# The ninth pair's up product by seven half products, weight sums of two pairs by DMA during the attention, and stores through GpSimd's queue

## The chip, the cores and the metric

The kernel runs on one core of one Trainium2 chip. The metric is device time in microseconds, from the start of the program to its end; before the change the runs took 647.18, 648.11 and 648.23 us, with a median of 648.11. TensorE (PE) multiplies; VectorE (DVE), ScalarE (ACT) and GpSimd (POOL) work elementwise; SyncE (SP) issues most DMAs. A DMA that GpSimd issues goes through a queue of its own, and it can add to its destination instead of overwriting it.

## The reference

One decoder layer over 512 tokens of width 1024, in float32:

```python
mix = fox_mixer(x, w_in, b_f, w_out)              # 16 heads of attention with forget gates
x = layer_norm(alpha * x + mix, g1, b1)
u, g = split(x @ w_up, 2816)                      # the up product: 1024 -> 2 x 2816
ffn = (gelu(causal_dwconv(g)) * u) @ w_down       # the down product: 2816 -> 1024
x = layer_norm(alpha * x + ffn, g2, b2)
out = x + sigmoid(x @ w_gate + b_gate) * (p @ w_proj)
```

Precision is kept by splitting each operand into a high and a low part (`hi` = the value rounded to the matmul's float32r form, `lo` = the rest) and adding three products: hi with hi, hi with lo, lo with hi.

## The kernel before, in words

**Stages.** The trace shows them in this order: the value, query and key projections with the attention, head by head (to about 226 us), the out projection and the first norm (to 247), the up and down products interleaved (247 to 566), the last down rows and the second norm (to 590), the gate with the embedding and the stores (to the end).

**Weights.** The class `Weights` holds a list of units, each up to 128x1024 numbers, in the order of their use. `load_to` issues a unit's load on SP's queue into one of four `raw` buffers (now and then into a piece of the tile `side`); `cut_to` splits it: ScalarE writes `whi` (L123), VectorE subtracts and writes `wlo` (L129), in five buffers each. `get(i, 4)` hands out unit i and first splits up to unit i + 4. A unit may have a `make`, sums of weights that VectorE forms before the split; `make` of the next unit runs ahead of the split of the present one.

**The up product in pairs.** F = 2816 is 22 rows of 128, in eleven pairs j = 0 to 10 (the "ninth pair" is j = 8, the "tenth" j = 9). For g and for u, a row done whole takes one unit and 24 products of 512 columns (`up`). A pair in `UP_PAIRS` takes a 2x2 block form with seven products of halves in place of eight (`up_step`): stages 0, 1, 2 are 24 products of 256 columns each, stage 3 is twelve, for g and u in turn. This form needs sums of x (`x_sums`, formed once, at L775) and four sums of the pair's weights. For pairs in `KEPT` (3, 4, 6, 7) VectorE forms these during the attention (`keep_sums`) and they are stored to DRAM (`keep_load`); for the other pairs in `UP_PAIRS` (2 and 9) VectorE forms them when the unit is due: `t12` two sums (L207, L208), `t3` one (L215), `t4` one (L222). Pairs outside `UP_PAIRS` need none.

**Operands of the down product.** After a pair's convolution and gate (`conv_product`: L759 to L768) its result E is summed (`operand_sums`, L855 to L858) and split (`operand_parts`, L863, L864) for the down product, which has a seven-product form as well, for three groups of three pairs (0 to 2, 3 to 5, 6 to 8). Where the next pair is in `APART`, this work waits until that pair's second unit; else it follows at once.

**The down product between the up units.** `down` yields twelve steps for a group: three each of ua, ub, uc, ud, one for each pair of the group. The first three kinds are twelve products of 512 columns, ud six; after the third of a kind, VectorE adds finished banks to the result (`give`, L661). `CHUNKS` says how many steps go to each of twelve (last group: eight) slots between the up units of the next group. The third step of a kind reads the operands of the group's last pair.

**Order.** From the up product's third row to the second norm, VectorE's and ScalarE's orders are the program's (`manual_schedule`). TensorE's order is made by a planner that takes, at each point of its own timeline, the first instruction of the program that it believes to be ready. A matmul that writes a bank waits until its last reader is done.

**Attention.** For each head, VectorE adds the mask and takes the maximum (L521), ScalarE exponentiates, GpSimd scales the four row blocks by the inverse sum (L533), and TensorE transposes them (L546) for the product with the values. GpSimd does nothing else there.

**The end.** `finish` forms a 128x512 piece of the output and stores it through SP's queue (L1107), which is also the queue of the gate weights' loads.

## Time and profile before

| | us |
|---|---|
| runs: 647.18, 648.11, 648.23, median | 648.11 |
| profiled execution | 648.06 |
| its span, first to last instruction | 646.4 |
| busy: TensorE / its weight loads / VectorE / ScalarE / GpSimd | 639.4 / 562.9 / 533.3 / 384.8 / 121.5 |
| DMA: 121.08 MB, mean rate | 187 GB/s |

A row of a group of instructions gives the line, the engine, the operation, what it writes and reads, the shape and count, then busy us and the mean in ns, and the idle time before it with what ended it. A row of a timeline begins with start and length in us. A matmul's length contains its way through the array; how often matmuls follow one another is read from their starts.

### The profile page before, as it was taken

The numbers are of one execution on the slowest core, as the hardware profiler recorded it, in microseconds if no ns is written. First come the engines' busy times: TensorE is split into PE (matmuls) and PEld (weight loads), VectorE is DVE, ScalarE is ACT, GpSimd is POOL, SyncE is SP. The second block draws the span as 40 slices with busy tenths as digits, with TensorE's granted clock in tenths as the row PEclk, the third lists the DMA queues.
The fourth block names the chain that finished last, engine by engine and source line by source line (L and its number), as shares of the span: only waits on it lengthen the run. The fifth ranks groups of instructions, "written<-read, shape, count | busy, mean of one in ns | idle before, by whom it ended". The sixth has DMA issues, their size and how long they took to land.

```text
span 646.4 us, 10081 instructions
## 1 busy us (share of the span) xinstructions
PE 639.4 (99%) x3630; PEld 562.9 (87%) x3630; DVE 533.3 (83%) x870; ACT 384.8 (60%) x685; POOL 121.5 (19%) x133
## 2 busy tenths in 40 slices
PE   9999999999999999999999999999999999999996
PEld 7899888888888889989999988999988998888885
DVE  7764779988888589857899897889797998699977
ACT  6643777877785316945756563646554555337863
POOL 0000554454456043110000010101010001002000
PEclk9999999999999999999999999999999999999999
DMA  8763525455588477685787849766846764671472
GB/s 296 239 235 131 204 83 175 166 186 158 178 280 305 133 254 219 137 209 156 198 223 160 223 128 247 196 204 149 249 132 184 192 213 143 167 243 33 139 228 98
DMA packets 49921, 121.08 MB, mean 187 GB/s; under 512 B 4880, under 2 KB 8720, under 8 KB 49872
## 3 DMA queue, kind: packets, MB, share of 16 engines
q1 hardware_dynamic: 45552, 108.92, 51.3%
q0 software_dynamic: 4320, 11.54, 10.6%
q8 instruction: 28, 0.46, 0.3%
q14 instruction: 21, 0.17, 0.1%
HBM read 107.72 MB, written 18.87 MB: 196 GB/s over the span
## 4 chain that ended last, share of the span: by engine, by line
PE 91%; DMA 3%; ACT 2%; DVE 2%; issue 1%; SPq 0%; ACTq 0%; DVEq 0%
PE g L152 18%; PE u L152 18%; PE pp L152 14%; PE x L152 8%; PE pv L152 7%; PE z L152 4%; PE r L152 3%; PE ap L152 3%; PE ao L152 3%; PE o L559 3%; PE t L546 3%; PE y L152 2%; PE s L509 2%; PE pl L152 2%; PE s L511 2%; DMA raw<-gt 2%
## 5 line engine op out<-in xcount | busy, mean ns | idle before, releaser
L123 ACT ACTIVATE whi<-raw 128x1024 fp32r<-128x1024 f32 (+4 forms) x141 | 132.6, 944 | 92.6 <-issue 12.9
L129 DVE TENSOR_TENSOR wlo<-raw,whi 128x1024 fp32r<-128x1024 f32 (+4 forms) x136 | 144.9, 1075 | 31.3 <-ACT whi L123 30.5
L533 POOL TENSOR_SCALAR pr<-pr,rl 128x128 f32<-128x128 f32 (+1 forms) x64 | 75.6, 1197 | 131.9 <-DVE rl L529 131.9
L280 POOL COPY neghalf<-neghalf 128x1 f32<-128x1 f32 x16 | 9.0, 562 | 247.0 <-ACT neghalf L279 247.0
L152 PE MATMUL g<-x1h,whi 128*128 128x256 f32 (+1 forms) x168 | 54.6, 325 | 0.0
L152 PE MATMUL g<-x1l,whi 128*128 128x256 f32 (+1 forms) x168 | 54.4, 324 | 0.0
L152 PE MATMUL g<-x1h,wlo 128*128 128x256 f32 (+1 forms) x168 | 54.3, 323 | 0.0
L152 PE MATMUL u<-x1l,whi 128*128 128x256 f32 (+1 forms) x160 | 52.9, 331 | 0.0
L152 PE MATMUL u<-x1h,wlo 128*128 128x256 f32 (+1 forms) x160 | 52.9, 331 | 0.0
L152 PE MATMUL u<-x1h,whi 128*128 128x256 f32 (+1 forms) x160 | 52.9, 331 | 0.0
L152 PE MATMUL pp<-xh,wlo 128*128 128x512 f32 x128 | 50.5, 395 | 0.0
L152 PE MATMUL pp<-xl,whi 128*128 128x512 f32 x128 | 50.0, 391 | 0.0
L152 PE MATMUL pp<-xh,whi 128*128 128x512 f32 x128 | 50.0, 390 | 0.0
L525 ACT ACTIVATE pr<-s,nm 128x128 f32<-128x128 f32 (+1 forms) x64 | 33.6, 528 | 9.1 <-DVE nm L521 8.9
L152 PEld LDWEIGHTS g<-x1h,whi 128*128 128x128 f32 x168 | 31.9, 190 | 3.4 <-issue 0.7
L152 PEld LDWEIGHTS g<-x1l,whi 128*128 128x128 f32 x168 | 31.9, 190 | 2.6
L152 PEld LDWEIGHTS g<-x1h,wlo 128*128 128x128 f32 x168 | 31.9, 190 | 2.6
L152 PEld LDWEIGHTS u<-x1h,whi 128*128 128x128 f32 x160 | 30.4, 190 | 3.0
L152 PEld LDWEIGHTS u<-x1l,whi 128*128 128x128 f32 x160 | 30.4, 190 | 2.9
L152 PEld LDWEIGHTS u<-x1h,wlo 128*128 128x128 f32 x160 | 30.4, 190 | 2.8
L123 ACT ACTIVATE whi<-side 128x512 fp32r<-128x512 f32 (+1 forms) x33 | 25.5, 782 | 11.0 <-DVE side L215 2.6
L521 DVE CUSTOM_DVE_ANT_0 s<-s,mask 128x128 f32<-128x128 f32 (+1 forms) x64 | 30.0, 512 | 1.7 <-PE s L511 1.5
(630 smaller groups left out, 1856.6 us busy)
## 6 DMA issues: line engine op xcount, KB each, us to landing
raw<-wup SPq DMA_DIRECT2D x34, 512.0 KB, 6.2
raw<-wdn SPq DMA_DIRECT2D x23, 512.0 KB, 4.6
raw<-wqk SPq DMA_DIRECT2D x16, 512.0 KB, 3.3
ka<-wup SPq DMA_DIRECT2D x8, 512.0 KB, 4.2
kb<-wup SPq DMA_DIRECT2D x8, 512.0 KB
kept<-kb SPq DMA_DIRECT2D x8, 512.0 KB, 3.4
kept<-ka SPq DMA_DIRECT2D x8, 512.0 KB, 3.1
raw<-wo SPq DMA_DIRECT2D x8, 512.0 KB, 4.4
```

Of the source, the lines that this page charges most:

```text
L123: self.nc.scalar.activation(hi[:, c:e], piece, AF.Copy)
L129: self.nc.vector.tensor_sub(lo[:, c:e], piece, hi[:, c:e].bitcast(F32))
L152: nc.tensor.matmul(ps, lhsT, rhs, start=start and n == 0, stop=stop and n == 2, skip_group_check=on)
L280: with tc.issue_after(nc.gpsimd.tensor_copy(small[:, m + 32:m + 33], small[:, m:m + 1]).ins):
L509: nc.tensor.matmul(ps[:, :n], QA[:, q], KA[:, :n], start=True, stop=False)
L511: nc.tensor.matmul(ps[:, :n], qb[0:68, q], kb[0:68, :n], start=False, stop=True)
L521: last_mask[:] = [nc.vector.tensor_tensor_reduce(ps[:, :w], ps[:, :w], mask[:, S - w:], -1.0, BIG, op0=ALU.add, op1=ALU.min, accum_out=nm[ ...
L525: nc.scalar.activation(pr[:, off:off + w], ps[:, :w], AF.Exp, bias=nm[:, i:i + 1], scale=-1.0, accum_out=ls[:, i:i + 1])
L533: nc.gpsimd.tensor_scalar_mul(pr[:, off:off + w], pr[:, off:off + w], rl[:, i:i + 1])
L546: nc.tensor.transpose(ps[:, w:w + P], pr[:, o:o + P], ident)
L559: nc.tensor.matmul(ps[:, q0:], V[:, j, h], p[:, o:o + w], start=j == 0 and n == 0, stop=j == NT - 1 and n == 1)
```

## The change

- Pair 8 joins `UP_PAIRS`: its up product takes the seven-product form. Pairs 8 and 9 join `APART`.
- Pairs 8 and 9 are in a new list `KEPT_DMA`. Their weight sums come from DRAM, like those of `KEPT`, but are formed by DMA: eight steps for each half of each pair, four copies and four accumulating DMAs of 256 KB, DRAM to DRAM. Two of these 32 are issued on GpSimd behind each head's scaling.
- An accumulating DMA only adds, so the signs of the weight sums of the up product turn from minus to plus, and the signs of the x sums and of one sum in stage 2 change to fit. Four x sums (two forms for two halves) and stage 2's add become `scalar_tensor_tensor`. The down product keeps its signs.
- The stores of `finish` go through GpSimd's queue, apart from the three of the last column half of the last two row tiles.

```diff
-UP_PAIRS = (2, 3, 4, 6, 7, 9)
+UP_PAIRS = (2, 3, 4, 6, 7, 8, 9)
 KEPT = (3, 4, 6, 7)
+KEPT_DMA = (8, 9)
-APART = (2, 3, 4, 7)
+APART = (2, 3, 4, 7, 8, 9)
...
-        if j in KEPT:
+        if j in KEPT + KEPT_DMA:
...
-            nc.vector.tensor_sub(b11, b12, b11)
-            nc.vector.tensor_sub(b12, b22, b12)
-            nc.vector.tensor_sub(b22, b22, b11)
-            last_sum[:] = [nc.vector.tensor_sub(b21, b21, b22).ins]
+            nc.vector.tensor_add(b11, b12, b11)
+            nc.vector.tensor_add(b12, b22, b12)
+            nc.vector.tensor_add(b22, b22, b11)
+            last_sum[:] = [nc.vector.tensor_add(b21, b21, b22).ins]
...
+    def keep_steps():
+        for js in [((j, 0), (j, 1)) for j in KEPT_DMA]:
+            for to, src, on in ((0, 0, 0), (3, 3, 0), (0, 2, 1), (2, 3, 0), (3, "t1", 1), (1, 1, 0), (2, 2, 1),
+                                (1, "t2", 1)):
+                for j, q in js:
+                    k = kept[j, q]
+                    b = k[:, {"t1": 0, "t2": 3}[src], :] if src in ("t1", "t2") else \
+                        wup[2 * j + src // 2, 1 - q][:, src % 2 * 4:src % 2 * 4 + 4]
+                    to_ap = k[:, to, :] if src in ("t1", "t2") else k[:, to, :].rearrange("p (a b) -> p a b", b=P)
+                    yield to_ap, b, on
+
+    keep_dma = keep_steps()
...
-            nc.gpsimd.tensor_scalar_mul(pr[:, off:off + w], pr[:, off:off + w], rl[:, i:i + 1])
+            scaled = nc.gpsimd.tensor_scalar_mul(pr[:, off:off + w], pr[:, off:off + w], rl[:, i:i + 1])
             off += w
+        with tc.issue_after(scaled.ins):
+            for to, src, on in itertools.islice(keep_dma, 2):
+                nc.gpsimd.dma_start(to, src, **(dict(accum_op=ALU.add) if on else {}))
...
-            nc.vector.tensor_add(s(0, i), blk(2 + i, 0), blk(2 + i, 1))
-            nc.vector.tensor_sub(s(1, i), s(0, i), blk(i, 0))
+            nc.vector.tensor_sub(s(0, i), blk(2 + i, 1), blk(2 + i, 0))
+            nc.vector.scalar_tensor_tensor(s(1, i), s(0, i), -1.0, blk(i, 0), op0=ALU.mult, op1=ALU.subtract)
             nc.vector.tensor_sub(s(2, i), blk(i, 0), blk(2 + i, 0))
-            nc.vector.tensor_sub(s(3, i), blk(i, 1), s(1, i))
+            nc.vector.scalar_tensor_tensor(s(3, i), blk(i, 1), -1.0, s(1, i), op0=ALU.mult, op1=ALU.subtract)
...
-            nc.vector.tensor_add(e[:, S:], ps, e[:, S:])
+            nc.vector.scalar_tensor_tensor(e[:, S:], ps, -1.0, e[:, S:], op0=ALU.mult, op1=ALU.subtract)
...
-        nc.sync.dma_start(out[t * P:(t + 1) * P, c0], y[:, t, c0])
+        (nc.sync if n == 0 and t in seconds else nc.gpsimd).dma_start(out[t * P:(t + 1) * P, c0], y[:, t, c0])
```

37 lines of the change are left out of this document (20 added, 17 removed).

## The prediction

> **What bounds the kernel now.** I read the page first, then who TensorE waits for, then a table of stretches, then the chain of waits pair by pair, and last each engine's list around the places that the change touches. The page's first line, its busy times, and the longest row of TensorE's list of waits:
>
> ```profile
> span 646.4 us, 10081 instructions
> ```
>
> ```profile
> PE 639.4 (99%) x3630; PEld 562.9 (87%) x3630; DVE 533.3 (83%) x870; ACT 384.8 (60%) x685; POOL 121.5 (19%) x133
> ```
>
> ```profile
> PE pl L152 <- DVE g22h L1147: 1.3, 1, 1.3
> ```
>
> TensorE has work nearly all the time; its longest wait is 1.3 us, close to the end. So time is won where TensorE gets less work or that wait goes, and lost where another engine becomes late. The stretches (length, then busy time of PE, PEld, DVE, ACT, POOL, the clock, the DMA share, GB/s) of the attention and of the ninth and tenth pair (j = 8 and 9; I go by j, so pair 7 is the one before them):
>
> ```profile
> 68.00:210.00 142.00, 141.93 (x761) 121.04 (x760) 120.41 (x272) 105.25 (x244) 75.59 (x64) 1.00 0.59 197
> 466.40:495.20 28.80, 28.80 (x128) 23.58 (x127) 23.28 (x35) 14.38 (x23) 3.02 (x4) 1.00 0.63 181
> 495.20:531.70 36.50, 36.50 (x241) 33.60 (x240) 35.90 (x55) 20.12 (x34) 2.21 (x4) 1.00 0.69 191
> ```
>
> The clock is full throughout. VectorE is the next bound: 35.90 of 36.50 us in pair 9, 23.28 of 28.80 in pair 8. The chain of waits (start, length, what):
>
> ```profile
> 435.24 2.88 PE g L152 x24
> 454.99 2.87 PE g L152 x24
> 462.12 1.36 PE z L152 x6
> 464.92 1.44 PE u L152 x12
> 474.55 5.44 PE u L152 x24
> 479.99 2.27 PE x L152 x10
> ```
>
> Products of 256 columns come 24 in 2.87 (0.120 us each), those of 512 columns 24 in 5.44 (0.227 us).
>
> **Pair 8's products.** Now: four units of 24 wide products, 4 x 5.44 = 21.76 us. After: for each of g and u 24 + 24 + 24 + 12 narrow ones, 2 x (3 x 2.87 + 1.44) = 20.1 us. TensorE wins 1.64 us, not an eighth of 21.76 (2.72), because a narrow product costs 53% of a wide one. The Trainium skill, "TensorE: Matmul & The Clock Gate", section "Back-to-back issue gap", gives 518 cycles for 512 columns and 262 for 256 at 2.4 GHz; by it the step would win 96 x 0.2158 - 168 x 0.1092 = 2.4 us (an estimate); the rows have both forms slower, so they decide.
>
> The whole-width form also has a bank wait, which the seven products don't have:
>
> ```profile
> 481.32 0.75 DVE L762 SCALAR_TENSOR_TENSOR a<-g,cw,a 128x510 f32<-128x510 f32 x1
> 481.86 0.39 PE L152 MATMUL x<-whi,b4h 128*128 128x512 f32 x1
> 482.22 0.47 PE L152 MATMUL g<-x1h,whi 128*128 128x512 f32 x1
> ```
>
> The next g starts at 482.22, 0.36 after the product before it, where 0.23 is the step: it needed the bank that L762 read until 482.07. Worth 0.13. These rows show something more. The run "x10" at 479.99 is a down step's six products and four of the next down step, which stands behind g in the program: the planner filled TensorE's wait with four later products (0.91 us) and was right to within 0.13 us. I use this below.
>
> **VectorE in pair 8.** It gains two wide and two half splits (six of 1.23 and two of 0.68 for four of 1.23: +3.8), four sums (2 x 0.42 and 2 x 0.75: +2.3), together +6.1 us. The conv and gate product of the whole-width form, which now fall mostly inside the pair, move behind its end. The place to look at is the third stage of pair 8. The model is pair 7, which already is in this form with the operand sums of the pair before it inside; VectorE's list there:
>
> ```profile
> 442.33 0.42 DVE L822 TENSOR_TENSOR side<-g,side 128x256 f32<-128x256 f32 x1
> 442.66 0.68 DVE L215 TENSOR_TENSOR side<-side 128x512 f32<-128x512 f32 x1
> ...
> 447.46 0.68 DVE L864 TENSOR_TENSOR a6l<-E,a6h 128x512 fp32r<-128x512 f32 x1
> ...
> 449.53 1.23 DVE L129 TENSOR_TENSOR wlo<-raw,whi 128x1024 fp32r<-128x1024 f32 x1
> ...
> 477.55 0.68 DVE L129 TENSOR_TENSOR wlo<-raw,whi 128x512 fp32r<-128x512 f32 x1
> 478.15 1.28 DVE L661 TENSOR_TENSOR y<-y,x 128x512 f32<-128x512 f32 x2
> 479.35 1.28 DVE L661 TENSOR_TENSOR y<-y,z 128x512 f32<-128x512 f32 x2
> ```
>
> In pair 7 the split for stage 2 of g ends at 450.76, 15.52 us behind the pair's first product (435.24), and is used at 19.75 (454.99): 4.2 us to spare. Pair 8 has other down steps between its stages: TensorE gets there after 2.88 + 2.73 + 2.87 + 1.36 + 2.87 + 2.88 + 1.36 = 16.95 us (two of them of one product, 1.36). VectorE has four adds more ahead of that split (L661, 2 x 1.28, less 0.1 by which such operations overlap in these rows: 2.4; 442.66 starts 0.09 before 442.33 + 0.42) and a half split in place of a whole one (0.68 - 1.23): 15.5 + 2.4 - 0.55 = 17.4. The third product is the first that reads wlo, 0.24 later than the first: TensorE is held 0.2 to 0.4 us. I take +0.3, bounds 0 and 0.6. The next weights are split behind it, so nothing can fill this wait.
>
> **From pair 8 to pair 9.** This is the dear place. Pair 9 is now in APART, so pair 8's operands are summed and split only inside pair 9, behind its second unit on VectorE's list; and pair 8's operands are read by the third down step already, two of them standing between pair 9's first units. In program order TensorE comes to the down step that reads pair 8's operands 2.88 + 4 x 1.36 + 2.88 = 11.2 us behind pair 9's first product. VectorE has, by pair 7's list, the first operand part done at 448.14, 12.9 behind the first product. Here three things are added: the two sums of a down weight, twice, and its two half splits, less the single sum of L215:
>
> ```profile
> L208 DVE TENSOR_TENSOR side<-raw 128x512 f32<-128x512 f32 x8 | 5.5, 692 | 0.3
> ```
>
> 2 x 1.38 + 2 x 0.68 - 0.68 = 3.4, some 0.1 less where they overlap: 16.2. The step is 5.0 us late. It costs that much if TensorE waits in program order. But the order of TensorE is the planner's, and there is work: stage 1 of pair 9's g (2.87; its split stands ahead of all these on VectorE's list) and the z half of the next down step (1.36). Both together take TensorE to 15.4, and 0.8 is left. I take +0.7, since the "x10" shows the planner filling to 0.13 us; bounds 0 and 5.0, and 2.1 if only g's stage is put in. Later in pair 9 VectorE is better off than before: it loses t12, t3 and t4 of both halves (8 x 0.69 = 5.5 us of 35.9).
>
> **Signs and sums.** tensor_sub against tensor_add is one operation on VectorE. Four sums of x, and one add in stage 2 of each of the fourteen unit pairs, become scalar_tensor_tensor: 0.75 (L762) against 0.69 for 512 elements, 0.06 us each, 1.1 us over all 18, spread over stretches with more to spare than that; 0, bound +0.2.
>
> **The sums by DMA in the attention.** 32 new DMAs of 256 KB, two behind each head's scaling on POOL: 16 copies, 16 accumulating. The rows of such DMAs that already run (first copies of 512 KB in 226 to 250, then accumulating ones of 256 KB in 383 to 490), of their issue, of POOL between its last two heads and of the transposes that wait for it:
>
> ```profile
> q0 software_dynamic: 1136, 4.16, 55.9%
> q0 software_dynamic: 1152, 2.10, 15.3%
> L281 POOL DMA_DIRECT2D gt<-gt x8 | 6.5, 818 | 0.7 <-issue 0.6
> 204.48 4.77 POOL L533 TENSOR_SCALAR pr<-pr,rl 128x128 f32<-128x128 f32 x4 [2.45 <-DVE rl L529]
> 210.66 0.60 PE L546 MATMUL t<-ident,pr 128*128 128x128 f32 x4
> DMA to landing us min/median/max: 4.6/5.7/8.7
> ```
>
> Engine time: 0.559 x 24 / 8 = 1.7 us for 512 KB copied, so 0.85 here; 0.153 x 107 / 9 = 1.8 for an accumulating one. 16 x 2.65 = 42 us over 142 lift the DMA share from 0.59 to 0.89. Two issues are 1.64 us of POOL, inside the 2.45 that it sits idle before the last head, whose scaling ends 1.41 us before its transposes. A step's predecessor is two heads (some 18 us) older and lands in 8.7 at most, so POOL doesn't stand. The keys' and queries' copies and the projections' weights queue behind more traffic; the nearest rows:
>
> ```profile
> 152.63 0.51 SPq L490 DMA_DIRECT2D KB<-KA  x1
> 161.42 0.28 PE L511 MATMUL s<-KB,QB 68*128 68x256 f32 x1
> ```
>
> 8.8 us from issue to use, 2.3 to land. I take 0; bounds 0 and +1.4 (the last head's slack spent).
>
> **Stores through POOL's queue.** The end, by engine:
>
> ```profile
> 620.88 0.94 SPq L1107 DMA_DIRECT2D out<-y  x2
> 622.66 0.33 SPq L93 DMA_DIRECT2D raw<-gt  x1
> 629.21 1.06 ACT L123 ACTIVATE whi<-raw 128x1024 fp32r<-128x1024 f32 x1 [2.99 <-DMA raw<-gt]
> 630.31 1.23 DVE L129 TENSOR_TENSOR wlo<-raw,whi 128x1024 fp32r<-128x1024 f32 x1 [2.22 <-ACT whi L123]
> 634.18 0.68 DVE L1147 TENSOR_TENSOR g22h<-g22h,pl 128x512 f32<-128x512 f32 x1
> ```
>
> Two stores of 256 KB are put in SP's queue just ahead of the last gate weight, which takes 6.5 us to land (622.66 to 629.2). ScalarE waits 2.99 for it, VectorE 2.22, and VectorE's list is then full until L1147, the row that TensorE's list of waits names with 1.3. With the stores in another queue the load no longer stands behind them, but still shares the 16 engines with them. If it lands as much earlier as VectorE waits, the whole 1.3 goes; if sharing costs the same as queueing, nothing. I take half, -0.7; bounds -1.3 and 0. "DMA: Bandwidth & Descriptors" of the Trainium skill, section "SWDGE vs HWDGE vs iDMA", says that the engines go round the queues in turn; no run yet shows it, and it speaks for a part and not the whole. A risk at the end: the last store on POOL is issued at about 640, and with POOL's 8.7 at worst it would land 2 us behind the span's end; at its 4.6 to 5.7, 1 us or more ahead of it. 0, bound +2.
>
> **Sum**, against the profiled execution's 648.06 (span 646.4 and 1.7 around it; the median of the runs is 648.11, the same): -1.64 - 0.13 + 0.3 + 0.7 - 0.7 = -1.5, so **646.6 us**.
>
> **Rivals.** (1) *The boundary wait takes the gain*: TensorE stands before the down step that reads pair 8's operands. For it: a list of VectorE of 16.2 us against 11.2. Against: the planner's fill. It decides from about 2.2 us of wait on; unfilled (5.0) the kernel is at 648.06 - 1.77 + 0.3 + 5.0 - 0.7 = 650.9, slower; with g's stage alone in it (2.1), 648.0. (2) *The stores change nothing*, since the load shares the engines anyway: 647.3, within what can't be told apart. (3) *The attention pays*, through a DMA share of 0.89 or POOL's last head: +1.4, 648.0. (4) *Everything fits*: no wait in pair 8 or behind it, all 1.3 of the end gone: 645.0.
>
> **Chances.** Forecast (646.6, own range 645.7 to 647.5) 0.45; rival 1 0.17, about half of it slower than before; rival 2 0.18; rival 3 0.10, a third of it slower; rival 4 0.10. A measurement of this kernel tells about 0.2% (1.3 us) from no change. Faster by more than that: rival 4, two thirds of the forecast's case, some of rival 2: 0.46. Slower: half of rival 1, parts of rival 3 and of a late last store: 0.18. Same: the rest, 0.36. The range, 644.9 to 649.4, reaches from rival 4 past rival 1 with g's stage alone, and leaves out its unfilled end.
>
> **What would show it.** Pair 8's 168 narrow products at 0.12 us each, and pair 8 about 1.3 us shorter. TensorE's list of waits should have a row for a split in pair 8's third stage (0.2 to 0.4) and one on pair 8's first operand part in pair 9 (0 to 1), with g's stage 1 ahead of that down step. If that row has 2 us or more, rival 1 holds. In the end, the wait on L1147 below 0.8 and ScalarE's wait for the last gate weight below 2.3 show the stores right; 1.3 and 3.0 show rival 2. New waits in the attention for POOL or the DMAs show rival 3. The forecast is wrong if pair 8 isn't shorter, or if the time leaves 645.7 to 647.5.

## The result, and the profile after

The changed kernel takes 651.17 us (median of 4 runs, 649.91 to 652.31) against 647.72 of the kernel before (4 runs, 647.18 to 648.23): ratio 1.0051, 95% interval 1.0029 to 1.0073. It is slower by half a per cent, where 646.6 us was forecast. Timed again later, it took 649.98 (6 runs) against 647.48: 1.0037, interval 1.0024 to 1.0051. The profiled execution is the fastest of the first four, 649.91 us.

The page's first lines and TensorE's waits after the change:

```profile
span 648.2 us, 10311 instructions
...
PE 638.8 (99%) x3702; PEld 564.7 (87%) x3702; DVE 533.8 (82%) x868; ACT 391.1 (60%) x701; POOL 148.9 (23%) x171
```

```profile
PE u L153 <- ACT whi L124: 1.5, 1, 1.5
PE x L153 <- ACT a8h L885: 1.1, 1, 1.1
...
PE pl L153 <- DVE g22h L1170: 0.4, 1, 0.4
```

TensorE's work is only 0.6 us less than before (639.4), although 1.64 us of products went; the wait at the end (L1170, which was L1147) fell from 1.3 to 0.4 us; and two waits are new, before pair 8's last u unit and on pair 8's first operand part (ScalarE's high half of it, L885). (All lines after the first inserted ones have moved by up to 23: L152 is L153, L129 is L130, L833 is L855, L864 is L886.)

Where the time stands is seen in the stretch from the first product of pair 7's last g unit (its stage 3) to the first product of pair 9's last g unit. It holds pair 8 whole, and the last units of pair 7 in place of those of pair 9, so as much work as two pairs; I call it "the two pairs". By stretches, first of the kernel before, then of the changed one (with the attention):

```profile
463.32:495.00 31.68, 31.68 (x152) 26.45 (x150) 25.23 (x36) 16.15 (x25) 3.02 (x4) 1.00 0.65 188
495.00:528.68 33.68, 33.68 (x218) 30.78 (x217) 33.05 (x52) 17.93 (x31) 2.21 (x4) 1.00 0.70 189
```

```profile
68.00:210.00 142.00, 141.90 (x761) 121.08 (x760) 120.17 (x272) 106.00 (x247) 96.34 (x95) 1.00 0.82 244
463.69:495.90 32.21, 30.61 (x224) 28.74 (x222) 25.56 (x37) 19.84 (x36) 2.47 (x4) 1.00 0.70 209
495.90:531.43 35.53, 34.40 (x219) 30.84 (x217) 33.40 (x49) 20.61 (x36) 3.48 (x4) 1.00 0.73 212
```

The two pairs took 65.36 us and now take 67.74: 2.4 us more, where the prediction had 0.8 less. VectorE isn't fuller there (25.56 and 33.40 against 25.23 and 33.05); ScalarE is busy 40.45 instead of 34.08.

### The profile page after: what moved, and what is told of

Its sections match the earlier page's. It is cut to its first block, busy times and chain, and to the rows that moved or that the text cites. A ratio compares the mean times of both kernels' runs of the same rounds, so it can differ in the third digit from the quotient of the medians.

```text
span 648.2 us, 10311 instructions
## 1 busy us (share of the span) xinstructions
PE 638.8 (99%) x3702; PEld 564.7 (87%) x3702; DVE 533.8 (82%) x868; ACT 391.1 (60%) x701; POOL 148.9 (23%) x171
## 3 DMA queue, kind: packets, MB, share of 16 engines
q0 software_dynamic: 8384, 21.50, 17.2%
## 5 line engine op out<-in xcount | busy, mean ns | idle before, releaser
L124 ACT ACTIVATE whi<-raw 128x1024 fp32r<-128x1024 f32 (+4 forms) x144 | 135.4, 945 | 95.0 <-issue 11.1
L130 DVE TENSOR_TENSOR wlo<-raw,whi 128x1024 fp32r<-128x1024 f32 (+4 forms) x139 | 148.4, 1077 | 37.5 <-ACT whi L124 36.5
L153 PE MATMUL g<-x1h,whi 128*128 128x256 f32 (+1 forms) x164 | 51.8, 316 | 0.0
L153 PE MATMUL u<-x1h,whi 128*128 128x256 f32 (+1 forms) x156 | 50.1, 321 | 1.5 <-ACT whi L124 1.5
L153 PE MATMUL g<-x1l,whi 128*128 128x256 f32 (+1 forms) x164 | 51.5, 314 | 0.0
L153 PE MATMUL g<-x1h,wlo 128*128 128x256 f32 (+1 forms) x164 | 51.5, 314 | 0.0
L153 PE MATMUL pp<-xh,wlo 128*128 128x512 f32 x128 | 50.4, 394 | 0.0
L153 PE MATMUL u<-x1l,whi 128*128 128x256 f32 (+1 forms) x156 | 50.1, 321 | 0.0
L153 PE MATMUL u<-x1h,wlo 128*128 128x256 f32 (+1 forms) x156 | 50.1, 321 | 0.0
L153 PE MATMUL pp<-xh,whi 128*128 128x512 f32 x128 | 50.0, 391 | 0.0
L153 PE MATMUL pp<-xl,whi 128*128 128x512 f32 x128 | 50.0, 390 | 0.0
L153 PEld LDWEIGHTS g<-x1h,whi 128*128 128x128 f32 x164 | 31.2, 190 | 2.4 <-issue 0.4
L153 PEld LDWEIGHTS u<-x1h,whi 128*128 128x128 f32 x156 | 29.7, 190 | 4.0 <-ACT whi L124 1.6
L153 PEld LDWEIGHTS g<-x1l,whi 128*128 128x128 f32 x164 | 31.2, 190 | 2.1
L153 PEld LDWEIGHTS g<-x1h,wlo 128*128 128x128 f32 x164 | 31.2, 190 | 1.9
L153 PE MATMUL g<-xsh,whi 128*128 128x256 f32 x112 | 31.7, 283 | 0.1
L153 PE MATMUL u<-xsh,whi 128*128 128x256 f32 x112 | 31.8, 284 | 0.0
L153 PEld LDWEIGHTS u<-x1l,whi 128*128 128x128 f32 x156 | 29.7, 190 | 2.4
L153 PE MATMUL u<-xsh,wlo 128*128 128x256 f32 x112 | 31.7, 283 | 0.0
```

The source lines that it names most:

```text
L124: self.nc.scalar.activation(hi[:, c:e], piece, AF.Copy)
L130: self.nc.vector.tensor_sub(lo[:, c:e], piece, hi[:, c:e].bitcast(F32))
L153: nc.tensor.matmul(ps, lhsT, rhs, start=start and n == 0, stop=stop and n == 2, skip_group_check=on)
```

## The experiments

For each profile four lengths are read: the start (to the first score product), the attention (from there to the first product of the output projection), the two pairs, and the tail (from the first product of the last down units to the end of the span).

| kernel | profiled, us | start | attention | two pairs | tail | runs: median (lowest to highest), ratio to before |
|---|---|---|---|---|---|---|
| before | 648.06 | 63.08 | 127.33 | 65.35 | 80.78 | |
| before_b | 649.73 | 65.69 | 127.21 | 65.35 | 80.29 | |
| before_c | 648.47 | 62.99 | 127.18 | 65.35 | 80.92 | |
| after | 649.91 | 63.83 | 127.29 | 67.74 | 79.88 | 651.17 (649.9 to 652.3), 1.0051 |
| after_b | 649.98 | 63.20 | 127.28 | 67.43 | 80.56 | 649.98 (649.7 to 651.0), 1.0037 |
| after_c | 649.98 | 63.45 | 127.77 | 67.63 | 79.94 | |
| no8 | 647.10 | 62.98 | 127.38 | 65.39 | 80.12 | 647.37 (646.8 to 648.7), 1.0003 |
| dmas_only | 647.83 | 63.47 | 128.33 | 65.39 | 79.47 | 647.58 (647.0 to 651.8), 1.0008 |
| half_dmas | 649.40 | 63.85 | 127.29 | 67.36 | 79.71 | 649.59 (649.2 to 651.0), 1.0033 |
| stores_only | 647.60 | 64.04 | 127.25 | 65.39 | 79.71 | 647.83 (646.5 to 649.5), 1.0002 |
| stores_sp | 654.93 | 63.52 | 130.89 | 68.27 | 80.32 | 653.26 (651.2 to 655.3), 1.0093 |
| sums_at_once | 648.90 | 63.62 | 128.47 | 65.81 | 79.85 | 649.75 (648.3 to 655.9), 1.0054 |
| evict_first | 647.28 | 63.31 | 127.33 | 65.61 | 79.76 | 652.28 (647.3 to 654.8), 1.0068 |
| evict_b | 649.59 | 64.06 | 127.19 | 67.11 | 80.00 | |
| combo | 654.50 | 63.88 | 128.63 | 70.61 | 80.20 | 653.82 (651.8 to 656.6), 1.0096 |
| gates_early | 649.09 | 64.01 | 127.26 | 66.85 | 79.61 | 648.85 (647.4 to 653.2), 1.0030 |
| both_at_once | 649.49 | 63.90 | 127.25 | 66.74 | 80.15 | 650.78 (648.4 to 654.1), 1.0064 |
| moved | 649.27 | 62.87 | 127.26 | 67.00 | 79.49 | 650.08 (649.3 to 651.4), 1.0052 |
| more_buffers_b | 646.80 | 63.02 | 127.43 | 65.71 | 79.43 | 647.46 (646.5 to 652.9), 1.0017 |

The start differs by up to 2.7 us between executions of one and the same kernel (the three of before), so a single time says less than the lengths. What the table leaves out differs less: 272.6 to 273.4 us from the output projection to the two pairs (274.05 in moved), and 36.90 from there to the tail in every profile.

### Pair 8 whole again: no8

```diff
-UP_PAIRS = (2, 3, 4, 6, 7, 8, 9)
+UP_PAIRS = (2, 3, 4, 6, 7, 9)
-KEPT_DMA = (8, 9)
+KEPT_DMA = (9,)
-APART = (2, 3, 4, 7, 8, 9)
+APART = (2, 3, 4, 7)
```

> Edit: pair 8 goes back to whole products with its operand sums as before, pair 9 keeps its weights' sums by DMA (16 DMAs in the attention in place of 32), the stores stay on GpSimd's queue. Theory A (the loss sits in pair 8 and in the border to pair 9, because seven products need more weights and more work of VectorE there): the end keeps its 0.9 us and everything else is as before, so 648.06 - 0.9 = 647.2 us, with pair 8 at 28.8 and pair 9 at 36.5 us or less (VectorE has 5.5 us less to do in pair 9). Rival B (the DMAs in the attention, or the start, cost something that the profiled run hid): it stays at 649 or above, with the excess ahead of the first pair.

Measured: ratio 1.0003 (0.9993 to 1.0012). Pair 8's seven products, with all that belongs to them, are what costs. The two pairs take 65.39 us as before. That VectorE has 5.5 us less to do in pair 9 brought nothing: TensorE's list of waits has no row there in the kernel before.

### The order of three lists: sums_at_once, evict_first, stores_sp

```diff
 sums_at_once:
-APART = (2, 3, 4, 7, 8, 9)
+APART = (2, 3, 4, 7, 8)
 evict_first:
-        hi, lo = W.get(u_up[j, st, s], 4)
+        hi, lo = W.get(u_up[j, st, s], 3 if (j, st, s) == (8, 2, 1) else 4)
 stores_sp:
-        (nc.sync if n == 0 and t in seconds else nc.gpsimd).dma_start(out...
+        nc.sync.dma_start(out...
```

> Edit: pair 8's operands are summed and split at once, before pair 9's units, and not behind its second unit (9 taken out of APART); all else as in the changed kernel. Theory (the place of the sums in VectorE's list makes the wait at the border): the first operand part, ready at 509.8 us in the changed kernel, is ready some 6 us earlier; the wait of 1.12 us for it goes, pair 9 takes 37 us in place of 38.4, and the kernel is 1.3 us shorter (profiled 648.6, median about 649.9). Rival (VectorE has too much there in any order): a split of pair 9 is late in its place, the wait changes its name, and the time stays within 0.4 us of the changed kernel's.

> Edit: in pair 8's stage 2 of u, the weights are looked ahead for by three units and not four, so that the sum that frees u's bank (L855) stands ahead of the split of pair 9's first weights in VectorE's list, and not behind it. Theory (TensorE's 1.5 us wait at u's stage 3 is this order: the sum waits behind a split whose weights came late): L855 of u runs as soon as its products end, the wait before u's stage 3 shrinks from 1.46 to under 0.3 us, pair 8 takes 27.9 us, and pair 9's first weights are split 0.7 us later, which their slack covers: the kernel is 1.0 to 1.5 us shorter. Rival (the late weights are what matters, the order only shows it): pair 9's first product waits instead, and the time stays within 0.4 us.

> Edit: all stores back on SyncE's queue; all else as in the changed kernel. Theory (moving the stores is what won the end 0.9 us): the wait for the last product's partner (L1170) goes back from 0.4 to about 1.3 us, ScalarE's wait for the last gate weight falls, as before the change, near 3 us, and the kernel is 0.9 us longer than the changed one (median about 652.0). Rival (the end differs by chance, or because everything ahead of it is later): 651.2, no difference.

The first two shorten the two pairs in their profiles, to 65.81 and 65.61 us, about as their theories said, but not their medians, and they spread over 7.5 us. In both the waits on L855 of u and on a8h are gone, and one on the bank of pair 9's first g has come:

```profile
PE g L153 <- ACT E L859: 0.9, 1, 0.9
```

That is evict_first; L859 is ScalarE's copy of pair 8's last g product, and on ScalarE's list it stands behind a split that waits for its load. In sums_at_once the same row has 0.5. In stores_sp the tail is 80.32, and the wait on L1170 0.7 us; but its profile lost 3.6 us in the attention, and 2.4 us at the same bank (the two pairs took 68.27), where its edit changes nothing. The loss in the attention led to the next two runs.

### What is the attention's share: dmas_only and half_dmas

```diff
 dmas_only (from no8):
-KEPT_DMA = (9,)
+KEPT_DMA = (8, 9)
 half_dmas (from the changed kernel):
-KEPT_DMA = (8, 9)
+KEPT_DMA = (9,)
...
+        if j in KEPT + KEPT_DMA + (8,):
+            kj = 7 if j == 8 else j
...
...
-                    lambda q: W.add(kept[j, q][:, 0:4:3, :], inner=512),
+                    lambda q: W.add(kept[kj, q][:, 0:4:3, :], inner=512),
...
```

> Edit: the kernel "no8" (pair 8 in whole products, 16 DMAs in the attention; 647.4 us, ten runs within 1.9 us of each other) with the other 16 DMAs put back: 32 in the attention, the sums of pair 8 made and not used. Theory A (the second 16 DMAs, beside the last heads and the loads of wo, make weights late there by an amount that changes from run to run: the profile of the kernel with the stores on SyncE's queue lost 3.6 us in the attention, that of "sums_at_once" 1.1, that of the changed kernel none): the runs spread over 3 us or more and the median is 648.5 to 650.5. Rival B (the 32 DMAs are covered, and the spread comes from pair 8's loads): 647.4 within 0.4, spread 2 us.

> Edit: the changed kernel with only pair 9's 16 DMAs in the attention; pair 8 has its seven products, but reads the sums that were made for pair 7, so the same loads of the same sizes with other values (the making of pair 8's sums is left out). Theory A (attention makes the spread; pairs 8 and 9 together cost 2.4 us more than before, 67.74 against 65.36 in the profiles, the end wins 0.7): no loss in the attention, spread about 2 us, median 648.5 to 649.5. Rival B (the loads of pair 8 make the spread): median near 651, spread over 3 us.

half_dmas, whose pair 8 is computed with the sums of pair 7, speaks for its theory: without pair 8's DMAs the spread is 1.9 us (seven runs), and 2.0 us of loss in the median are left, which is what its two pairs show (67.36 against 65.35). dmas_only decides for neither: the median didn't move (1.0008, 0.9992 to 1.0023), but its profile lost 1.1 us in the attention, and single runs took 649.0 and 651.8. TensorE's row in dmas_only, then ScalarE and TensorE in stores_sp, where the same wait is longest, and ScalarE at that place in the kernel before:

```profile
PE s L528 <- DVE PTl L572: 1.0, 1, 1.0
```

```profile
155.68 1.06 ACT L124 ACTIVATE whi<-raw 128x1024 fp32r<-128x1024 f32 x1 [2.15 <-DMA raw<-wo]
...
164.40 0.50 PE L528 MATMUL s<-KA,QA 128*128 128x512 f32 x1 [2.01 <-DVE PTl L572]
```

```profile
153.12 1.06 ACT L123 ACTIVATE whi<-raw 128x1024 fp32r<-128x1024 f32 x1
```

A weight of the output projection lands late in the profiles that lose; ScalarE stands 2.15 us before its split, the softmax of that head is queued behind it on the same engine, VectorE gets the transposes late, and TensorE waits for their bank. Before the change the same split had no wait. That the DMAs of the last heads make the weight late is argued from the count that follows, not shown by a run. Eleven profiles have the changed kernel's 32 DMAs in the heads: eight have the attention at 127.2 to 127.8 us, three at 128.3, 128.5 and 130.9; the mean is 0.6 us above the 127.27 of the others that have no DMA or 16 there.

### The lot together: combo

```diff
+    keep_some(nc.gpsimd.tensor_copy(small[:, 60:61], logits[NT - 1][:, :1]).ins, 14)
...
-        hi, lo = W.get(u_up[j, st, s], 4)
+        hi, lo = W.get(u_up[j, st, s], 3 if (j, st, s) in ((8, 2, 1), (8, 3, 0), (8, 3, 1)) else 4)
-APART = (2, 3, 4, 7, 8, 9)
+APART = (2, 3, 4, 7, 8)
```

> Edit: the changed kernel with (1) pair 8's DMAs issued one behind the other from the end of the first value rows on (16 to 68 us, where the DMA engines are 30 to 70% busy) and only pair 9's in the first heads, (2) the evictions of pair 8's stages 2 and 3 ahead of the splits of pair 9's weights (look-ahead of three units), (3) pair 8's operand sums at once (9 out of APART). Theory: no loss in the attention, no wait of over 0.5 us in pairs 8 and 9, which together take 64.0 to 64.8 us (65.36 before): 645.5 to 646.8, faster than before by 0.1 to 0.3%. Rival (VectorE and the loads have no room for the seven products in any order, the wait moves on): pairs 8 and 9 at 65.4 or more, 647 or above.

Both parts failed. The early DMAs met a copy of keys in the first heads (a wait of 1.3 us for KB), and in the two pairs pair 8's operand parts now stand ahead of the split of pair 9's u weights on ScalarE's list: TensorE waited 2.77 us until 507.15, and had half its clock until about 513.5 (shown in the last section). The two pairs took 70.61 us. Each list order buys one wait with another; which of the remedies lost most here wasn't tried apart.

### The stores alone, and the profiles of before again: stores_only, before_b, before_c

```diff
-        nc.sync.dma_start(out[t * P:(t + 1) * P, c0], y[:, t, c0])
+        (nc.sync if n == 0 and t in seconds else nc.gpsimd).dma_start(out[t * P:(t + 1) * P, c0], y[:, t, c0])
```

> Edit: the kernel before with the stores of the output on GpSimd's queue as in the changed kernel, nothing else. Theory (prediction's step): the wait for L1147 falls from 1.3 to 0.5 us, 0.7 us shorter: ratio 0.9989. Rival ("no8", which has this too, measures 1.0003, so the stores win nothing in the median): 1.000, with the last gate weight landing as late as before.

> Edit: none, the kernel before again, for a second profile: "stores_only" ended 1.1 us sooner after its last FFN product than the profile of before, and its median is the same. Theory A (the profiled execution of before had an unusually long wait at its end, 1.3 us, and a start that was 0.5 to 1 us quicker than in the other profiles): here the wait for L1147 is below 1 us and the first scores come at 63.4 to 64.0 us in place of 63.1. Rival B (the stores win 0.7 us and something else in that kernel pays it back): wait 1.2 to 1.5 us again.

> Edit: none, the kernel before a third time, for its profile: the same as for the second.

TensorE's wait at the end in stores_only, in before_b and in before_c:

```profile
PE pl L152 <- DVE g22h L1147: 0.3, 1, 0.3
```

```profile
PE pl L152 <- DVE g22h L1147: 0.8, 1, 0.8
```

```profile
PE pl L152 <- DVE g22h L1147: 1.5, 1, 1.5
```

With the stores on SyncE's queue the tail is 80.3 to 80.9 us (4 profiles, mean 80.58), with GpSimd's 79.4 to 80.6 (15 profiles, mean 79.86): 0.7 us, the size forecast. The ranges overlap, and the ten runs of stores_only (1.0002, 0.9991 to 1.0013) and of no8 don't show it. So the profiles speak for the prediction's step and the medians for rival 2; before_c says that 1.3 to 1.5 us of wait are usual there, before_b that they aren't always. Whether the stores are worth 0.7 us or next to nothing stays open.

### The changed kernel again: after_b, after_c

> Edit: none, the changed kernel again, for a second profile and more times. Theory (pairs 8 and 9 always cost some 2 us more than before, as in "half_dmas", 649.6 us; the 32 DMAs in the attention and the late weights add a further part that changes from run to run): median 650 to 651.5, spread of 3 us or more; the profile has the waits at u's stage 3 and at pair 8's first operand part (1 to 2 us together), and what it loses beyond 649.6 stands in the attention (at the scores near 163 us) or in pairs 8 and 9. Rival (the first four times were high by chance): median 649.6 or below, spread 2 us.

> Edit: none, the changed kernel a third time, for its profile: the same as for the second.

```profile
PE u L153 <- DVE E L855: 1.2, 1, 1.2
PE pl L153 <- DVE g22h L1170: 1.1, 1, 1.1
PE x L153 <- ACT a8h L885: 1.1, 1, 1.1
```

This is after_b; after_c has 1.4 and 1.1 on u and x. The loss in the two pairs is no accident of one run: 67.4 to 67.7 us in all three profiles.

### Why the weights are late: the lists

The rows that lead to the waits at stage 2 of g and at u are in the lists of VectorE, SyncE, ScalarE and TensorE of the changed kernel:

```profile
482.74 1.22 DVE L130 TENSOR_TENSOR wlo<-raw,whi 128x1024 fp32r<-128x1024 f32 x1
...
487.84 0.68 DVE L855 SCALAR_TENSOR_TENSOR E<-g,E 128x512 f32<-128x512 f32 x1
492.42 1.22 DVE L130 TENSOR_TENSOR wlo<-raw,whi 128x1024 fp32r<-128x1024 f32 x1 [3.90 <-ACT whi L124]
493.56 0.68 DVE L855 SCALAR_TENSOR_TENSOR E<-u,E 128x512 f32<-128x512 f32 x1
```

```profile
475.98 3.32 SPq L94 DMA_DIRECT2D raw<-kept  x2
483.98 0.33 SPq L94 DMA_DIRECT2D raw<-wup  x1
```

```profile
480.45 1.06 ACT L885 ACTIVATE s7h<-E 128x1024 fp32r<-128x1024 f32 x1 [3.36 <-DVE E L880]
...
483.66 0.37 ACT L849 ACTIVATE E<-g 128x256 f32<-128x256 f32 x1
...
491.33 1.06 ACT L124 ACTIVATE whi<-raw 128x1024 fp32r<-128x1024 f32 x1 [4.22 <-PE x L153]
```

```profile
483.67 0.28 PE L153 MATMUL u<-xsh,wlo 128*128 128x256 f32 x1
484.09 0.38 PE L153 MATMUL g<-xsh,whi 128*128 128x256 f32 x1
...
484.43 0.28 PE L153 MATMUL g<-xsh,wlo 128*128 128x256 f32 x1
...
494.39 0.36 PE L153 MATMUL u<-x1h,whi 128*128 128x256 f32 x1 [1.46 <-ACT whi L124]
```

TensorE stands 0.30 us before stage 2 of g (484.09 behind 483.67, where a step is 0.12), the length that was forecast. But it doesn't stand there for VectorE's split, which runs from 482.74 to 483.96. The product that waits is the first, and that reads `whi`; the first that reads `wlo`, the third, starts at 484.43, 0.47 us after the split's end. It waits for ScalarE's copy of the bank (L849, done at 484.04), and so says the profile of L849, under who waited for it:

```profile
  PEld g L153: 0.3, 1
```

ScalarE is late because it stood 3.36 us for the operand sums of pair 7 on VectorE's list (L880), with two whole splits between that wait and the copy.

The late split does its harm elsewhere. It is the last reader of a load buffer: the load of pair 9's first weights is issued at 483.98, 0.02 us later. It isn't split before 491.33. ScalarE stands 4.22 us (the row names TensorE, whose x products run at that moment; but the `whi` that this split writes was last read by stage 2 of g, whose products end by 487.3, and the last of the load's 16 parts landed at 491.23 by the trace, so it is the load), VectorE 3.90; and the sum that frees u's bank, L855, has its place behind that split on VectorE's list. TensorE stands 1.46 us before u's last unit.

The DMA engines' share over 480 to 497 us, in 40 slices of 0.425 us:

```profile
DMA  4943000000489589898989899999999997569976
```

They are idle from about 482 to 484.2 and full from 486 to 494. Nothing is short of bandwidth before 484: there is no free buffer to load into, and then six loads are issued within 4 us.

### Two DMAs fewer, sums at once, DMAs elsewhere: gates_early, both_at_once, moved, evict_b

```diff
 gates_early:
-            if f >= 6:
+            for _ in range(2 if f in (10, 11) else 0 if f in (16, 17) else f >= 6):
                 next(beside)
 both_at_once:
-APART = (2, 3, 4, 7, 8, 9)
+APART = (2, 3, 4, 7)
 moved (from sums_at_once):
-KEPT_DMA = (8, 9)
+KEPT_DMA = (9, 8)
...
+            keep_some(2 if h < 8 else 0)
...
                     nc.gpsimd.dma_start(quad(to, k, 1), quad(src, k, 1), accum_op=ALU.add)
+                    keep_some(2)
```

> Edit: the two gate sums by DMA that stand in pair 8's two halves are issued with those of pair 5; no DMA on GpSimd's queue in pair 8. Theory A (these accumulating DMAs, whose packets run at 484 to 487 us, make the load of pair 9's first weights late, 7.3 us from issue to landing): the load lands 2 us sooner, ScalarE's 4.2 us wait before pair 9's first split falls to near 2, the wait before u's stage 3 goes, pairs 8 and 9 take 66.1 us in place of 67.5 (median 648.6). Rival B (the load is late because its buffer comes free late and the loads ahead of it share the engines in any case): pairs 8 and 9 within 0.4 us of 67.5, median 650.

> Edit: 8 and 9 taken out of APART: the operands of pair 7 are summed ahead of pair 8's units, those of pair 8 ahead of pair 9's. Theory A (VectorE's list between stage 0 of u and stage 2 of g of pair 8 is what is too long; its splits there free the buffers late, and the loads that wait for them come back late 7 us on): with pair 7's sums out of that place, the split for stage 2 of g ends 2 us sooner, pair 9's first weights are loaded 2 us sooner, the waits at stage 2 of g and at stage 3 of u go, pairs 8 and 9 take 64.6 to 65.4 us (65.8 with pair 8's alone at once), median 647.5. Rival B (the work only changes its place): waits in pair 8's first stages in their stead, pairs 8 and 9 at 65.8 or more.

> Edit: "sums_at_once" with pair 8's 16 DMAs taken out of the last eight heads and issued two at a time behind the first eight gate sums (pairs 3 to 6). Theory A (the spread of that kernel, 648.3 to 655.9 us, comes from the attention, where its profile lost 1.2 us): attention at 127.3 us, pairs 8 and 9 at 65.8, the runs within 2.5 us of each other, median 647.6 to 648.2. Rival B (the spread comes from late loads in pairs 8 and 9): spread over 4 us again, median near 649.8.

> Edit: none, "evict_first" again, for a second profile: its ten times lie between 647.3 and 654.8 us (median 652.3), and the profile is that of the fastest. Theory A (with a look-ahead of three units the weights of pair 9 are loaded so late that in most runs TensorE waits for them in pairs 8 and 9, as in "combo", 70.6 us for the two pairs): pairs 8 and 9 take 68 to 71 us, with a row of waits for ScalarE's whi. Rival B (the DMAs in the attention): pairs 8 and 9 at 65.6 again, the attention 129 to 133 us in place of 127.3.

Without the gate sums in pair 8 the load, issued at 484.23, is split 0.9 us sooner than in the changed kernel, and the two pairs take 66.85, 0.6 to 0.9 less. That speaks for contention as a part, and the smaller one; it is one profile, and the same load's landing varies more than that between runs of one program (below). ScalarE there, in a row that names the load:

```profile
490.39 1.06 ACT L124 ACTIVATE whi<-raw 128x1024 fp32r<-128x1024 f32 x1 [3.03 <-DMA raw<-wup]
```

With both operand sums at once a new wait stands two units earlier, before stage 1 of g, where the sums now hold up VectorE's list:

```profile
478.08 0.39 PE L153 MATMUL g<-xsh,whi 128*128 128x256 f32 x1 [2.55 <-DVE E L844]
```

So VectorE has no room for pair 7's sums there either, rival B. In moved the attention is at its 127.26 and the spread falls to 2.2 us in four runs, but the DMAs cost 1.4 us in the pairs ahead of pair 8, and the two pairs take 67.0. evict_b, the same program as evict_first, shows one reason why that kernel spreads, and it is neither of the two expected cases: ScalarE's split of the same weights, first in evict_first and then in evict_b:

```profile
486.95 1.06 ACT L124 ACTIVATE whi<-raw 128x1024 fp32r<-128x1024 f32 x1 [0.23 <-PE g L153]
```

```profile
491.48 1.06 ACT L124 ACTIVATE whi<-raw 128x1024 fp32r<-128x1024 f32 x1 [4.21 <-PE x L153]
```

Its load, from SyncE's list of the one and the other:

```profile
483.59 0.33 SPq L94 DMA_DIRECT2D raw<-wup  x1
```

```profile
484.14 0.33 SPq L94 DMA_DIRECT2D raw<-wup  x1
```

It was there after at most 3.4 us in evict_first and took some 7.3 in evict_b, with the same loads around it; the two pairs differ by 1.5 us (65.61, 67.11).

### One buffer more: more_buffers, more_buffers_b

```diff
-        more = any(u in self.more for u in range(self.cut, self.cut + RAW_BUFS))
-        self.load_to(self.cut + RAW_BUFS - (not more))
+        n = raws = self.cut
+        while raws < self.cut + RAW_BUFS:
+            raws += n not in self.more
+            n += 1
+        self.load_to(min(n - 1, self.cut + 5))
...
+    for u in range(u_up[0, 1] + 7, len(W.units), 5):
+        if u > u_up[3, 0, 0]:
+            W.more[u] = lambda: aside[0][:, 3:5, :].rearrange("p a b -> p (a b)")
```

> Edit: the changed kernel with one more buffer for loaded weights from pair 3 on: two of the side blocks (3 and 4), which only the sums of pairs 2 and before use now, take every fifth unit, so that loads run one unit further ahead; nothing else is changed. Theory A (pair 9's first weights are late because their buffer comes free late, behind VectorE's long list): they are issued some 2 to 5 us sooner, ScalarE's wait of 4.2 us before the first split of pair 9 falls below 2, the 1.5 us wait of u's stage 3 goes, and pairs 8 and 9 take 65.3 to 66.3 us in place of 67.5: median 648 to 648.7. Rival B (the DMA engines have no more to give in pair 8, so loads issued sooner land as late): 67.2 to 67.7 again, median 650.

> Edit: as "more_buffers", with the look-ahead of the loads held to five units, so that no block of side is loaded again before the unit in it has been split (in "more_buffers" it was, and those loads and splits stood behind each other). Theory A (pair 9's first weights are late because their buffer comes free late, behind VectorE's long list): they are issued 2 to 5 us sooner, ScalarE's wait of 4.2 us before the first split of pair 9 falls below 2, the 1.5 us wait of u's stage 3 goes, and pairs 8 and 9 take 65.3 to 66.3 us in place of 67.5: median 648 to 648.7. Rival B (the DMA engines have no more to give in pair 8, so loads issued sooner land as late): 67.2 to 67.7 again, median 650.

In more_buffers the bound of five units was missing, so loads were put over weights not yet split; the splits and loads stood behind each other, and its 685 us say nothing of the question. In more_buffers_b, by the order of the program, the further buffer is still taken some units before pair 2's last halves have read it, so those halves are computed from other values; the instructions, their sizes and their order from pair 3 on are as meant. SyncE, ScalarE, VectorE and TensorE there:

```profile
475.33 0.33 SPq L94 DMA_DIRECT2D raw<-wup  x1
```

```profile
486.54 1.06 ACT L124 ACTIVATE whi<-raw 128x1024 fp32r<-128x1024 f32 x1
```

```profile
487.78 1.21 DVE L130 TENSOR_TENSOR wlo<-raw,whi 128x1024 fp32r<-128x1024 f32 x1
489.49 0.69 DVE L861 SCALAR_TENSOR_TENSOR E<-u,E 128x512 f32<-128x512 f32 x1 [0.49 <-PE u L156]
```

```profile
507.18 0.50 PE L156 MATMUL x<-whi,a8h 128*128 128x512 f32 x1 [0.53 <-ACT a8h L891]
```

Pair 9's first weights are loaded 8.0 us sooner, counted from the start of the two pairs (475.33 against 483.98 in the two lists, and this kernel is 0.65 ahead), neither ScalarE nor VectorE waits for them, u's sum is done by 490.18, and the wait at u is gone. The two pairs take 65.71 in place of 67.4 to 67.7, and the median is 647.46 against 647.14 (1.0017, 0.9992 to 1.0043). Theory A holds: a buffer that is freed late was the cause of some 2 us, with no engine's list shortened. The run also shows what is left without that cause: 0.29 us before stage 2 of g, again behind ScalarE's copy, and 0.69 before the step that reads pair 8's operands (the wait of 0.53 and the slower start of the product).

No version beats the kernel before. The nearest, stores_only, no8, dmas_only and, of those with pair 8's seven products, more_buffers_b alone, can't be told from it.

## Why the prediction was wrong, step by step

- **Pair 8's products, -1.64**: right in size. The two pairs have 168 products of 256 columns and 198 of 512 before, 336 and 102 after; at the 0.1198 and 0.227 us that they take back to back, 65.07 and 63.41 us. The bank wait of the whole-width form (0.13, part of the 0.28 us that the two pairs take above 65.07) is gone as forecast, but the new form has small waits of its own, below.
- **VectorE in pair 8's third stage, +0.3**: a wait of 0.30 us stands where it was put, but not for the reason given, so the number is luck. The split ends 17.4 us behind the pair's first product (483.96 and 466.56), as worked out; TensorE got there only at 17.2 instead of 16.95, and by these rows the third product would have found the split done. What TensorE waits for is ScalarE's copy of the bank, and ScalarE's list isn't in the prediction's sum. (The wait is 0.28 to 0.32 in most other kernels of this form, 0.08 in gates_early, and absent in both_at_once.) **This is the step that failed**, and with its last sentence, "The next weights are split behind it, so nothing can fill this wait", it cost most: it asked who waits for the late split and not what the split sets free, a load buffer, and so put the loads at nothing. The load behind it was issued 0.02 us after the split, was split itself up to 7.3 us later, and held up ScalarE, VectorE and, through a bank, TensorE: 1.46 us in this profile, 1.2 and 1.4 in the two others, and about 0.6 more of what follows in pair 9. more_buffers_b, which changes this alone, gets 1.7 to 2.0 us back.
- **From pair 8 to pair 9, +0.7**: 1.12 us of wait, 1.28 with the slower first product. The planner filled it with half of stage 1 of g (1.4 us), not with the 4.2 us that the forecast put there. With the late load taken away the place costs 0.69, the forecast's own number, but here too the terms differ: TensorE waits for ScalarE's high half of the operand (a8h, done at 509.8, 13.9 us behind pair 9's first product), while VectorE's low half came at 514.0, 18.1 behind where 16.2 was worked out, and the planner bridged that with other products. So the agreement is in part luck. The other 0.6 belongs to the step above, because VectorE's list came into pair 9 late. Rival 1 named the right place, but neither of its prices, 2.1 or 5.0 us, was seen.
- **Small steps, not in the sum**: in more_buffers_b the two pairs are 2.30 us above the 63.41 of their products; 0.98 are the two waits, and about 1.1 is in nine places of 0.1 to 0.2, where the kernel before has 0.28 in all (65.35 against 65.07): short waits for banks at 475.96, 493.74 and 510.74, and a product after a wait that is itself 0.10 to 0.11 slower. So even with loads on time the form wins nothing over 65.35.
- **VectorE relieved in pair 9**: true and worth nothing (no8: 65.39).
- **Signs**: nothing; nothing in the profiles points at them.
- **The attention's DMAs, 0, bounds 0 and +1.4**: 0 in the changed kernel's own profile (127.29), at a DMA share of 0.82 where 0.89 was worked out (the working divides by nine accumulating DMAs where its window holds eight; with eight it gives 0.92). But single executions lose 1.1, 1.2 and 3.6 us, 0.6 in the mean over eleven profiles, and one is above the upper bound. The bound came from POOL's slack at the last head; the loss came from a weight of the output projection and ScalarE's list. Rival 3 was right in part.
- **The stores, -0.7**: 0.7 in the mean of the tails, nothing in the medians. Of the two signs that were named, the wait on L1170 fell below 0.8 in this profile and in after_c (0.4 and 0.5) but not in after_b (1.1); ScalarE's wait for the last gate weight (3.44) is no shorter. SyncE's and ScalarE's rows after the change:

```profile
625.37 0.32 SPq L94 DMA_DIRECT2D raw<-gt  x1
```

```profile
631.06 1.06 ACT L124 ACTIVATE whi<-raw 128x1024 fp32r<-128x1024 f32 x1 [3.44 <-PE pl L153]
```

That load is split 5.7 us behind its issue instead of 6.5, and ScalarE's work ahead of it ends sooner too, so the wait is long though the load is early.

In sum: -1.66 for the products, +0.3, +0.7 and -0.7 as forecast, and on top 1.7 to 2.0 us of late loads, 1.0 of small steps (less what was there before) and 0.6 of attention in the mean: 1.9 to 2.2 us above 648.06, or about 650. That is where after_b and after_c stand, though a single execution needn't follow the means: after_b lost nothing in the attention (127.28) and won 0.2 in the tail (80.56), not 0.7. The two slower of the first four runs have no profile; the slowest, 652.31, had a granted clock of 0.996 (see the last section), the other, 651.73, one of 0.999, and what that one lost can't be said.

The Trainium skill, "Perfetto Trace Analysis", section "Optimization Strategies", advises to look at those engines that block the critical path when TensorE waits. Here the trace agrees only at one remove: VectorE was as free in the two pairs as before, and what stood between it and its next work was a buffer.

## What to carry to other kernels

When an engine's list gets later, follow each late instruction in two directions: who waits for its result, and what it sets free. A load that waits for the buffer starts then, and comes back a landing time later, 3.4 to 7.3 us here, as a wait with another engine's name on it. Idle DMA slices just ahead of full ones are the sign to look for, and one more buffer is the test. Here a gain of 1.66 us in products was outweighed by 1.7 to 2.0 us of late loads. And see what the waiting instruction reads and writes before a cause is named: here a wait of the forecast length in the forecast place had another one.

## What the runs showed of the hardware that was not expected

A wait can cost more than its length: beside some waits of about 2 us TensorE's granted clock falls to half. The clock is the column behind POOL's. In stores_sp behind the 2.01 us that end at 164.40, in combo with the 2.77 us that end at 507.15 (it falls before they end), and in before_b, in the first value products, behind a wait of 1.94 us that ends at 10.27:

```profile
164.40:166.40 2.00, 2.00 (x8) 1.73 (x9) 2.00 (x9) 0.92 (x4) 2.00 (x2) 0.92 1.01 414
166.40:169.80 3.40, 3.40 (x10) 2.58 (x10) 3.23 (x8) 2.02 (x5) 2.62 (x5) 0.55 0.61 152
169.80:175.00 5.20, 5.20 (x33) 4.59 (x32) 1.40 (x3) 2.52 (x6) 4.62 (x5) 1.00 1.03 225
```

```profile
507.20:509.00 1.80, 1.65 (x4) 1.26 (x5) 1.80 (x3) 1.77 (x4) 0.91 (x2) 0.50 0.28 25
509.00:511.00 2.00, 2.00 (x10) 1.90 (x10) 2.00 (x4) 1.65 (x2) 0.00 (x0) 0.50 0.96 84
511.00:515.00 4.00, 4.00 (x21) 3.78 (x20) 2.48 (x4) 2.03 (x4) 0.00 (x0) 0.69 0.91 264
```

```profile
10.70:13.90 3.20, 3.20 (x16) 3.20 (x16) 2.91 (x5) 2.31 (x5) 0.00 (x0) 0.50 1.04 402
```

In combo the clock is at half until about 513.5 (0.69 over the last 4 us is 2.5 us at half). The kernel before has 28 products from 10.70 to 13.90 where before_b has 16; with the wait, which is 0.43 us in the kernel before, that is about the 2.6 us by which before_b's start is longer.

Products of 512 columns take 0.43 us each in the slow stretch of stores_sp:

```profile
166.50 0.63 PE L153 MATMUL pp<-xh,whi 128*128 128x512 f32 x1
166.93 0.63 PE L153 MATMUL pp<-xh,wlo 128*128 128x512 f32 x1
167.36 0.63 PE L153 MATMUL pp<-xl,whi 128*128 128x512 f32 x1
```

Eight of them at 0.20 us too much are 1.6 us on top of a wait of 2.0. Behind the 2.55 us wait of both_at_once the clock stayed at 1.00, so the length of the wait alone doesn't decide. The Trainium skill, "TensorE: Matmul & The Clock Gate", section "Part 1: The HAM clock gate (the "warmup" mystery)", has the clock halved after an idle window of some 3.4 us, and the windows run on freely whenever the work begins. The slow stretch of 3.4 us in stores_sp and the dependence on more than the length agree with that; but the waits beside which the clock fell here, 1.9, 2.0 and 2.8 us, are shorter than the window, and for how long a wait may be the measurement decides.

The same load of 512 KB, issued at the same place of the same program among the same other loads, landed within 3.4 us in one execution and took 7.3 in the next (evict_first and evict_b), and the two pairs differed by 1.5 us. The times of evict_first lie 7.5 us apart, and the granted clock of each run tells part of the rest: its four runs at 0.999 or 1.0 took 647.28 to 651.86 us, the six at 0.994 to 0.997 took 652.25 to 654.82. All 19 runs above 652 us among the versions of the table have 0.997 or less, and in the kernel before the only two above 649 us, 649.73 (before_b) and 650.12, have 0.997. So much of the spread goes with lost clock, and a version that makes TensorE wait some 2 us can pay for it twice. Which wait came before the loss in the runs without a profile can't be said.
